# The first layer's row vectors, low halves, modulation sums and spatial gating in another order

## The chip, the core and the metric

The kernel runs on one core of one Trainium2 chip, as one program. The metric is device microseconds for one execution. Engines: PE is TensorE, DVE VectorE, ACT ScalarE, POOL GpSimd, SP SyncE, which issues nearly all DMAs. PSUM holds eight banks of 128 partitions by 512 floats.

## What is computed

The reference is a network of two blocks on 512 tokens of width 1024, with a context of 256 tokens. The first block has two layers. Only its first layer matters here ("ab" in the code), which runs on the tokens and, with the same weights, on the context:

```python
m = silu(c) @ w_mod + b_mod            # sh, sc, gt: 3 x 1024; once for c, once for c_ctx
h = x * (1 + sc) + sh                  # 512 tokens, and 256 of the context
z = h @ w_in                           # a, ga, u, v, gb: 5 x 512
ya = pool(a) * silu(ga)                # window sums over tokens, a 128x128 product per group, a scale
vn = per-head layer norm of v          # 4 heads of 128
yb = u * (w_s @ vn + b_s) * silu(gb)   # spatial gating, w_s 128x128 per head, in chunks of 128 tokens
x = layer_norm(ALPHA * x + gt * (concat(ya, yb) @ w_out))
```

The second layer ("cd": Fourier mixing and attention) takes its modulation `silu(c) @ w_mod` from the same c, with weights of its own. The second block is two rounds of a gated feed-forward, a mixing layer with three kinds of attention, and a second feed-forward.

## The kernel before, in words

**Layout and precision.** Activations lie with channels on partitions, `[128, 8, 512]`; the first layer's 768 tokens are 512 of x (tile `X`, high and low half) and 256 of the context (`C`). Every large product is three matmuls (`mm3`, L144): a number is split into a rounded high half and the rest, and high times high, high times low and low times high are added. A tile of weights, 128x1024 floats, is loaded by `wload` (L74) on SP into `ws` (two buffers), its high half is made by ScalarE (L92), and its low half by the engine `s.w_eng` (L93). `wnext` (L127) takes the next weight and loads up to four ahead; there are five buffers of high and low halves. In the first two layers `s.w_eng` is GpSimd, set at L517 and set back to VectorE at L1075.

**Jobs.** `wload` also works off a list `s.jobs`: for each weight loaded it adds `s.rate` (2.2) to a count and runs a job for each whole one (L94 to L97). In the first layer the jobs are the modulations that aren't needed at once: rows 16 to 23 of the first layer's (the gate gt) and all 24 of the second layer's. One job (`mod_dve`, L468) loads a 512 KB tile of weights into one of the spare buffers and has VectorE multiply it by a row of silu(c) laid out over all partitions and sum it up (L475), once for c and once for c_ctx, or once only.

**The order.** The source gives the dependences and a priority; the build works out from them one fixed order for each engine and for SP's queue. An instruction whose inputs are due early may so stand before ones that are written ahead of it, as far as its buffers allow. At run time no engine leaves its order.

**The first layer.** `ab` (L514) works in stages:

- Modulation and the projection of v, to about 64 us. For each of eight channel tiles k, `mods(k)` (L540) computes the rows k and 8+k of the modulation: on TensorE for the rows in `ON_PE` (eight small products and a bias, L548, L549), on VectorE with `mod_dve` for the others. `modx(k)` (L554) scales x. Then 18 matmuls with `ab_v` add tile k's share into six banks `pv`. The rows of silu(c) that `mod_dve` needs are loaded as `crow`, 2 x 512 KB, the same in each partition (L562 to L565).
- The norm of v (L598 to L610): six copies out of PSUM by ScalarE, 24 `bn_stats` and `bn_aggr`, one `rsqrt` of eight small steps (L194 to L202), and 24 instructions that subtract the mean and scale, all on VectorE.
- Spatial gating, g = 0 to 3 (L625 to L647). One projection (`proj`, L612) is 24 matmuls of 512 columns into one bank and 24 of 256 into a second one; the six `mm` banks hold three projections. The order is u of 0, gb of 0, u of 1, then for each g the product `pf` of vn and w_s into the two `t` banks (L637), the sum with b_s (L642), the product with u (L644), with silu of gb (L645), and the split into the halves of Y (L646).
- Pooling, g = 0 to 3 (L658 to L700): projections a and ga, window sums by repeated addition (L668), corrections at the edges, the difference with a (L681), its split, the product `pp` with pool_w (L689), taken one group later, the scale (L691) and a split.
- All remaining jobs, the biases of both modulations and the second layer's `gb` (L702 to L715).
- The output: eight tiles of 24 + 24 matmuls, added to x by VectorE (L508), with token sums on GpSimd (L512); the last three by segments, then the layer norm (L487), interleaved with these.

`mod_dve`'s buffers for jobs are parts of `xs` and `ctmp` that lie idle (L580 to L585, L652).

Of the kernel before, what the change touches and what calls it, by code (L numbers as in the profile page):

```python
# [9 lines left out]
F32 = mybir.dt.float32  # L10
# [3 lines left out]
ALU = mybir.AluOpType  # L14
# [7 lines left out]
ALPHA = 4.0 ** 0.25  # L22
ON_PE = (0, 8, 10, 13, 15)
HALF = (slice(0, 256), slice(256, 512))
# [7 lines left out]
class Net:  # L32
# [415 lines left out]
    def ab_weights(s):  # L448
        I = s.I
        for c in range(4):  # L450
            s.wpush(I["ab_v"][c], 1024)
        for i in (8, 12, 9, 13, 10, 14, 11, 15):
            s.wpush(I["ab_in"][i], 1024)
        s.wpush(I["pool_w"], 512)
        for i in (0, 4, 1, 5, 2, 6, 3, 7):
            s.wpush(I["ab_in"][i], 1024)
        for m in range(8):
            s.wpush(I["ab_out"][m], 1024)
# [55 lines left out]
    def ab(s):  # L514
        nc, tc, I = s.nc, s.tc, s.I
        s.psum(mm=range(6), t=(6, 7))
        s.w_eng = nc.gpsimd  # L517
        fbt = s.xp.tile([P, 4096], F32, tag="fb", name="fbt")
# [5 lines left out]
        C = [c_p.tile([P, 8, 256], F32R, tag="c" + t, name="c" + t) for t in "HL"]  # L524
        s.mods_start()
        b1 = c_p.tile([P, 16], F32, name="b1")
        nc.vector.tensor_copy(b1[:, 0:8], s.vec("ab_b", 0, 8))
        nc.vector.tensor_scalar(b1[:, 8:16], s.vec("ab_b", 8, 8), 1.0, None, op0=ALU.add)
        xs = s.xp.tile([P, 4096], F32, tag="x", name="xs")
        pv = [s.bank("pv") for _ in range(6)]  # L530

# [22 lines left out]
        def modx(k):  # L554
            st = xs[:, k % 5 * 768:k % 5 * 768 + 768]
            nc.sync.dma_start(st, I["x"][:, k])
            s.modulate(X, k, ALL, st[:, :T], s.ab_m[:, 8 + k, 0:1], s.ab_m[:, k, 0:1], st[:, :T])
            s.modulate(C, k, slice(0, 256), st[:, T:], s.ab_m[:, 8 + k, 1:2], s.ab_m[:, k, 1:2], st[:, T:])
# [3 lines left out]
        for v in range(2):  # L562
            row = fbt[:, v * 1024:(v + 1) * 1024]
            nc.sync.dma_start(row, I["crow"][:, v * 1024:(v + 1) * 1024])
            nc.scalar.activation(row, row, AF.Silu)  # L565
        modx(0)
        mods(1)
        for k in range(8):
            if k % 2 == 0:
                W = s.wnext(1)  # L570
            if k < 7:
                modx(k + 1)
            if k < 6:
                mods(k + 2)
            w = [x[:, k % 2 * T:(k % 2 + 1) * T] for x in W]
            for t in range(6):
                s.mm3(pv[t], tokx(k, t), w, k == 0, k == 7)
        mx.close()
        ctmp = c_p.tile([P, 2048], F32, tag="cx", name="ctmp")
        spare = []  # L580

        def buf():
            spare.append(spare.pop(0))
            return spare[-1]
        spare += [xs[:, 3072:], ctmp[:, :1024], ctmp[:, 1024:]]  # L585
        nc.sync.dma_start(s.ident, I["ident"])
        nc.sync.dma_start(fbt[:, 2048:2560], I["sgu_b"])
# [3 lines left out]
        with tc.tile_pool(name="y", bufs=1, reuse_waits="tile") as yp, tc.tile_pool(name="yt", bufs=1, reuse_waits="tile") as tp:  # L591
# [14 lines left out]
            rv = s.rsqrt(ve, 24, "sgu")  # L606
            for t in range(6):
                for h in range(4):
                    j = t * 4 + h
                    nc.vector.tensor_scalar(vn[:, t, h], vn[:, t, h], mv[:, j, 0:1], rv[:, j:j + 1], op0=ALU.subtract, op1=ALU.mult)  # L610

# [12 lines left out]

            u = proj()  # L625
            for g in range(4):
                gb = proj()
                if g < 3:
                    u2 = proj()
                if g == 0:  # L630
                    s.jobs = [(lambda i=i: s.mod_dve(s.ab_m, I["ab_mod"], i, 2, fbt, buf)) for i in range(16, 24)]
                    s.jobs += [(lambda i=i: s.mod_dve(s.cd_m, I["cd_mod"], i, 2 if i < 16 else 1, fbt, buf)) for i in range(24)]
                G = tp.tile([P, 768], F32, tag="G", name="G")
                t_ = tp.tile([P, 768], F32, tag="T", name="T")
                pf = s.bank("pf", "t"), s.bank("pf", "t")
                for c in range(6):
                    nc.tensor.matmul(pf[c // 4][:, c % 4 * P:(c % 4 + 1) * P], vn[:, c, g], fbt[:, 2560 + g * P:2560 + (g + 1) * P], start=True, stop=True)  # L637
                for i, sl in enumerate(PARTS):
                    n = sl.stop - sl.start
                    bs = fbt[:, 2048 + g * P:2048 + (g + 1) * P].unsqueeze(1).to_broadcast([P, n // P, P])  # L640
                    tt = t_[:, sl]
                    nc.vector.tensor_tensor(tt.rearrange("p (c i) -> p c i", i=P), pf[i][:, :n].rearrange("p (c i) -> p c i", i=P), bs, op=ALU.add)  # L642
                    nc.scalar.activation(G[:, sl], gb[i], AF.Silu)
                    nc.vector.tensor_tensor(tt, tt, u[i], op=ALU.mult)  # L644
                    nc.vector.tensor_tensor(tt, tt, G[:, sl], op=ALU.mult)  # L645
                    ysplit(4 + g, tt, sl)  # L646
                u = u2  # L647


            LP = 800  # L650
            A, S1, S2 = ctmp[:, 0:LP], ctmp[:, LP:2 * LP], fbt[:, 3072:3072 + LP]
            spare[:] = [xs[:, j * 1024:(j + 1) * 1024] for j in range(4)]  # L652
            nc.gpsimd.memset(ctmp, 0.0)
# [47 lines left out]

            while s.jobs:  # L702
                s.jobs.pop(0)()
            s.add_bias(s.ab_m, "ab_b", 16, 24)

            nc.vector.tensor_scalar(s.ab_m[:, 16:24], s.ab_m[:, 16:24], 1.0 / ALPHA, None, op0=ALU.mult)
            s.add_bias(s.cd_m, "cd_b", 0, 16)
            s.add_bias(s.cd_m, "cd_b", 16, 24, 1)
            nc.vector.tensor_scalar(s.cd_m[:, 8:16], s.cd_m[:, 8:16], 1.0, None, op0=ALU.add)

            s.gb = s.fc.tile([P, 2, 8, 2], F32, name="gb")
            for v in range(2):
                nc.vector.tensor_tensor(s.gb[:, 0, :, v], s.cd_m[:, 8:16, v], s.vec("ab_g", 0, 8), op=ALU.mult)
                nc.vector.tensor_tensor(s.gb[:, 1, :, v], s.cd_m[:, 8:16, v], s.vec("ab_lb", 0, 8), op=ALU.mult)
                nc.vector.tensor_tensor(s.gb[:, 1, :, v], s.gb[:, 1, :, v], s.cd_m[:, 0:8, v], op=ALU.add)  # L715
            ag = c_p.tile([P, 2, 8], F32, name="ag")
# [22 lines left out]
            for m in range(5):  # L739
                W = s.wnext()  # L740
                a, b = s.bank("pa"), s.bank("pb")[:, :256]
                omm(a, W, slice(0, T))
                omm(b, W, slice(T, 768))
                fin(m, 0, a[:, 0:256])
                fin(m, 1, a[:, 256:512])
                fin(m, 2, b)
            Ws = s.wlast(3)

# [751 lines left out]
def prep_first(inp, A, vec):  # L1500
    i = lambda n: inp[n][0]
    cc = np.stack([i("c"), inp["c_ctx"]])
    vec("c", np.ascontiguousarray(cc.reshape(2, 8, P).transpose(2, 1, 0)).reshape(P, 16))
    A["crow"] = np.ascontiguousarray(np.broadcast_to(cc.reshape(1, 2048), (P, 2048)))
    vec("ab_b", rows(i("ab_b_mod")))
# [130 lines left out]
```

## Time and profile before

| | us |
|---|---|
| median of 3 runs | 2746.2 |
| the runs | 2743.26, 2746.2, 2751.51 |
| the profiled execution's own time | 2743.77 |
| its span in the trace | 2741.7 |

In the profile TensorE is busy for 2632.7 us (96% of the span), VectorE for 1504.3, ScalarE for 1056.6, GpSimd for 323.0. A line of a timeline gives start, duration, engine, source line, operation, output<-inputs and, in brackets, how long the engine was idle before and what ended that. Matmul durations overlap: the pitch of two is shorter than one. DVE_READ_ACCUMULATOR rows belong to the sum before them. In the first 350 us the trace has 34 low halves on GpSimd and 78 sums on VectorE.

### The profile page before, as it was taken

How to read it: one execution, taken by the hardware profiler on the slowest of the kernel's cores; microseconds unless marked ns; L12 is line 12 of the kernel's file. 1: busy time of each engine (PE TensorE's matmuls, PEld its weight loads, DVE VectorE, ACT ScalarE, POOL GpSimd, SP SyncE). 2: the span in 40 equal slices, each digit the busy share in tenths (PEclk: the TensorE clock that was granted, in tenths of full speed). 3: DMA queues.
4: the chain of work that ended last, by engine and by line, in shares of the span. 5: the costliest groups of instructions: out<-in, count | busy, mean ns of one | idle time of the engine just before them, and what ended most of it. 6: DMA issues, size and time to landing. Idle time of an engine off the chain costs nothing. (4 is left out here: it accounts for less than half of the span.)

```text
span 2741.7 us, 36211 instructions
## 1 busy us (share of the span) xinstructions
PE 2632.7 (96%) x13676; PEld 2230.8 (81%) x13676; DVE 1504.3 (55%) x2886; ACT 1056.6 (39%) x1951; POOL 323.0 (12%) x300
## 2 busy tenths in 40 slices
PE   7898999998999999999999999999999998999998
PEld 6787987887888888878888888888888877988887
DVE  7895632888545345675853336633336666642434
ACT  4122533664444233454543224432223454432222
POOL 2323344003000011001200002000001001200000
PEclk9999999998999999999999999999999999999999
DMA  7353123004998247654693323963237655232221
GB/s 271 135 193 120 44 82 101 32 30 166 312 315 291 91 141 234 195 154 140 219 317 109 99 84 108 318 221 100 92 101 243 208 156 156 76 100 99 94 94 60
DMA packets 133966, 418.15 MB, mean 153 GB/s; under 512 B 17376, under 2 KB 20960, under 8 KB 133792
## 3 DMA queue, kind: packets, MB, share of 16 engines
q1 hardware_dynamic: 133792, 415.84, 45.7%
q8 instruction: 108, 1.77, 0.3%
q14 instruction: 66, 0.54, 0.1%
HBM read 314.32 MB, written 73.40 MB: 141 GB/s over the span
## 5 line engine op out<-in xcount | busy, mean ns | idle before, releaser
L92 ACT ACTIVATE wh<-ws 128x1024 fp32r<-128x1024 f32 (+2 forms) x335 | 345.3, 1033 | 865.4 <-PE pd L148 238.6
L93 DVE TENSOR_TENSOR wl<-ws,wh 128x1024 fp32r<-128x1024 f32 (+1 forms) x267 | 318.3, 1192 | 164.4 <-ACT wh L92 161.1
L147 PE MATMUL pg<-xH,wh 128*128 128x512 f32 x672 | 262.2, 390 | 0.0
L149 PE MATMUL pg<-xH,wl 128*128 128x512 f32 x672 | 261.7, 389 | 0.0
L148 PE MATMUL pg<-xL,wh 128*128 128x512 f32 x672 | 261.6, 389 | 0.0
L149 PE MATMUL pd<-hH,wl 128*128 128x512 f32 x632 | 249.6, 395 | 0.0
L147 PE MATMUL pd<-hH,wh 128*128 128x512 f32 x632 | 249.6, 395 | 0.0
L148 PE MATMUL pd<-hL,wh 128*128 128x512 f32 x632 | 249.6, 395 | 0.0
L148 PE MATMUL pu<-xL,wh 128*128 128x512 f32 x640 | 249.2, 389 | 0.0
L147 PE MATMUL pu<-xH,wh 128*128 128x512 f32 x640 | 249.1, 389 | 0.0
L149 PE MATMUL pu<-xH,wl 128*128 128x512 f32 x640 | 249.0, 389 | 0.0
L93 POOL TENSOR_TENSOR wl<-ws,wh 128x1024 fp32r<-128x1024 f32 (+1 forms) x68 | 171.5, 2529 | 326.1 <-ACT wh L92 317.0
L247 POOL TENSOR_TENSOR accf<-accf,sq 128x256 f32<-128x256 f32 x48 | 39.7, 847 | 1390.1 <-ACT sq L246 1390.1
L399 DVE TENSOR_TENSOR ht<-ht,pu 128x512 f32<-128x512 f32 x80 | 54.9, 686 | 182.5 <-PE pu L149 180.4
L149 PEld LDWEIGHTS pg<-xH,wl 128*128 128x128 f32 x672 | 126.1, 188 | 26.1
L148 PEld LDWEIGHTS pg<-xL,wh 128*128 128x128 f32 x672 | 126.2, 188 | 26.0
L147 PEld LDWEIGHTS pg<-xH,wh 128*128 128x128 f32 x672 | 126.2, 188 | 26.1
L148 PEld LDWEIGHTS pd<-hL,wh 128*128 128x128 f32 x632 | 118.6, 188 | 28.8
L149 PEld LDWEIGHTS pd<-hH,wl 128*128 128x128 f32 x632 | 118.6, 188 | 28.8
L147 PEld LDWEIGHTS pd<-hH,wh 128*128 128x128 f32 x632 | 118.6, 188 | 28.7
L147 PEld LDWEIGHTS pu<-xH,wh 128*128 128x128 f32 x640 | 120.1, 188 | 25.0
L148 PEld LDWEIGHTS pu<-xL,wh 128*128 128x128 f32 x640 | 120.1, 188 | 24.9
(622 smaller groups left out, 5982.6 us busy)
## 6 DMA issues: line engine op xcount, KB each, us to landing
ws<-ffn_gate SPq DMA_DIRECT2D x88, 512.0 KB, 3.5
ws<-ffn_up SPq DMA_DIRECT2D x88, 512.0 KB, 3.5
hl<-eh SPq DMA_DIRECT2D x64, 512.0 KB, 6.8
hl<-el SPq DMA_DIRECT2D x64, 512.0 KB, 6.8
ws<-ffn_down SPq DMA_DIRECT2D x64, 512.0 KB, 3.6
wh<-hl SPq DMA_DIRECT2D x58, 512.0 KB, 4.3
wl<-hl SPq DMA_DIRECT2D x58, 512.0 KB, 6.0
es<-wqk SPq DMA_DIRECT2D x32, 512.0 KB, 5.8
```

The source lines that it names most:

```text
L92: nc.scalar.activation(wh[:, :n], st[:, :n], AF.Copy)
L93: s.w_eng.tensor_tensor(wl[:, :n], st[:, :n], f(wh[:, :n]), op=ALU.subtract)
L147: mm(out, A[0], B[0], start=start, stop=False)
L148: mm(out, A[0], B[1], start=False, stop=False)
L149: mm(out, A[1], B[0], start=False, stop=stop)
L247: (eng or nc.gpsimd).tensor_tensor(acc[0], acc[0], sq, op=ALU.add)
L399: nc.vector.tensor_tensor(t, t, pu, op=ALU.mult)
```

## The change

It has six parts. `ON_PE` gets eight rows instead of five (rows 1, 9, 12 and 14 come in, 13 goes out). Low halves of the first two layers are made by VectorE. The rows of silu(c) are made on TensorE: sixteen products of a column of silu(c), taken as a weight matrix of equal columns, with the identity, copied out of four banks by ScalarE; the load of `crow` goes, the identity is loaded at the start. The scale of v by its norm goes head by head and is shared: odd token tiles on ScalarE, even ones on VectorE; the jobs' VectorE instructions are tied behind the last one on VectorE (`issue_after`), have three buffers of their own and a rate of 1.4. The spatial gating's product, sum and product with u of group g stand ahead of the projection gb of g, and the projections come as u0, u1, gb0, u2, gb1, u3, gb2, gb3. Up to 24 jobs and the second layer's `gb` may come behind the first five output tiles.

```diff
-ON_PE = (0, 8, 10, 13, 15)
+ON_PE = (0, 1, 8, 9, 10, 12, 14, 15)
@@ ab_weights
-        for i in (8, 12, 9, 13, 10, 14, 11, 15):
+        for i in (8, 9, 12, 10, 13, 11, 14, 15):
             s.wpush(I["ab_in"][i], 1024)
@@ ab
-        s.w_eng = nc.gpsimd
+        s.w_eng = nc.vector
...
         s.mods_start()
+        nc.sync.dma_start(s.ident, I["ident"])
...
-        pv = [s.bank("pv") for _ in range(6)]
...
         for v in range(2):
-            row = fbt[:, v * 1024:(v + 1) * 1024]
-            nc.sync.dma_start(row, I["crow"][:, v * 1024:(v + 1) * 1024])
-            nc.scalar.activation(row, row, AF.Silu)
+            for h in range(2):
+                pr = s.bank("pr")
+                for j in range(4):
+                    nc.tensor.matmul(pr[:, j * P:(j + 1) * P], s.sc[:, 4 * h + j, v:v + 1].to_broadcast([P, P]), s.ident, start=True, stop=True)
+                nc.scalar.activation(fbt[:, v * 1024 + h * T:v * 1024 + (h + 1) * T], pr, AF.Copy)
         modx(0)
+        s.wload(1)
         mods(1)
+        pv = [s.bank("pv") for _ in range(6)]
...
-        spare = []
-        def buf():
-            spare.append(spare.pop(0))
-            return spare[-1]
-        spare += [xs[:, 3072:], ctmp[:, :1024], ctmp[:, 1024:]]
-        nc.sync.dma_start(s.ident, I["ident"])
+        buf = lambda: c_p.tile([P, 1024], F32, tag="mj", name="mj", bufs=3)
...
             rv = s.rsqrt(ve, 24, "sgu")
-            for t in range(6):
-                for h in range(4):
+            nb = c_p.tile([P, 24], F32, name="nb")
+            nc.vector.scalar_tensor_tensor(nb, mv[:, :, 0], -1.0, rv, op0=ALU.mult, op1=ALU.mult)
+            for h in range(4):
+                for t in range(6):
                     j = t * 4 + h
-                    nc.vector.tensor_scalar(vn[:, t, h], vn[:, t, h], mv[:, j, 0:1], rv[:, j:j + 1], op0=ALU.subtract, op1=ALU.mult)
+                    if t % 2:
+                        nc.scalar.activation(vn[:, t, h], vn[:, t, h], AF.Identity, scale=rv[:, j:j + 1], bias=nb[:, j:j + 1])
+                    else:
+                        normed = nc.vector.tensor_scalar(vn[:, t, h], vn[:, t, h], mv[:, j, 0:1], rv[:, j:j + 1], op0=ALU.subtract, op1=ALU.mult)
...
-            u = proj()
+            def after_v(*a):
+                def run():
+                    with tc.issue_after(normed.ins):
+                        s.mod_dve(*a, fbt, buf)
+                return run
+            us = [proj(), proj()]
+            s.jobs = [after_v(s.ab_m, I["ab_mod"], i, 2) for i in range(16, 24)]
+            s.jobs += [after_v(s.cd_m, I["cd_mod"], i, 2 if i < 16 else 1) for i in range(24)]
+            s.rate = 1.4
             for g in range(4):
-                gb = proj()
-                if g < 3:
-                    u2 = proj()
-                if g == 0:
-                    s.jobs = [(lambda i=i: s.mod_dve(s.ab_m, I["ab_mod"], i, 2, fbt, buf)) for i in range(16, 24)]
-                    s.jobs += [(lambda i=i: s.mod_dve(s.cd_m, I["cd_mod"], i, 2 if i < 16 else 1, fbt, buf)) for i in range(24)]
-                G = tp.tile([P, 768], F32, tag="G", name="G")
-                t_ = tp.tile([P, 768], F32, tag="T", name="T")
                 pf = s.bank("pf", "t"), s.bank("pf", "t")
...
+                t_ = tp.tile([P, 768], F32, tag="T", name="T")
                 for i, sl in enumerate(PARTS):
...
                     nc.vector.tensor_tensor(tt.rearrange("p (c i) -> p c i", i=P), pf[i][:, :n].rearrange("p (c i) -> p c i", i=P), bs, op=ALU.add)
+                    nc.vector.tensor_tensor(tt, tt, us[g][i], op=ALU.mult)
+                gb = proj()
+                if g < 2:
+                    us.append(proj())
+                G = tp.tile([P, 768], F32, tag="G", name="G")
+                for i, sl in enumerate(PARTS):
                     nc.scalar.activation(G[:, sl], gb[i], AF.Silu)
-                    nc.vector.tensor_tensor(tt, tt, u[i], op=ALU.mult)
-                    nc.vector.tensor_tensor(tt, tt, G[:, sl], op=ALU.mult)
-                    ysplit(4 + g, tt, sl)
-                u = u2
+                    nc.vector.tensor_tensor(t_[:, sl], t_[:, sl], G[:, sl], op=ALU.mult)
+                    ysplit(4 + g, t_[:, sl], sl)
...
-            spare[:] = [xs[:, j * 1024:(j + 1) * 1024] for j in range(4)]
...
-            while s.jobs:
+            while len(s.jobs) > 24:
                 s.jobs.pop(0)()
             s.add_bias(s.ab_m, "ab_b", 16, 24)
...
                 fin(m, 2, b)
+            while s.jobs:
+                s.jobs.pop(0)()
```

Behind the last two lines stand, unchanged, the biases of the second layer's modulation and its `gb`, which stood behind the pooling before.

## Rows read from the trace of the kernel before

**Rows 1.** The page, its first line: the span and the number of instructions

```profile
span 2741.7 us, 36211 instructions
```

**Rows 2.** Busy time by stretch (us), instructions as (x), TensorE's granted clock, DMA share, GB/s

```profile
64.00:149.00 85.00, 77.51 (x422) 66.47 (x421) 66.83 (x148) 17.56 (x26) 31.90 (x12) 0.92 0.42 148
97.10:101.70 4.60, 4.58 (x12) 3.09 (x11) 4.50 (x8) 0.00 (x0) 0.00 (x0) 0.50 0.19 47
149.00:224.90 75.90, 72.78 (x417) 63.87 (x416) 73.07 (x117) 19.21 (x35) 19.94 (x7) 0.98 0.55 188
224.90:245.20 20.30, 10.16 (x46) 8.17 (x45) 16.32 (x20) 5.83 (x11) 7.86 (x3) 0.75 0.48 159
245.20:290.00 44.80, 44.80 (x283) 40.31 (x284) 9.62 (x22) 5.85 (x8) 19.41 (x17) 1.00 0.20 66
331.00:690.00 359.00, 341.34 (x1979) 293.41 (x1979) 221.07 (x481) 188.63 (x403) 92.94 (x63) 0.97 0.24 82
```

**Rows 3.** TensorE's timeline, 78 to 113 us: start, duration, line, tiles, [idle before <-releaser]

```profile
80.49 0.39 PE L147 MATMUL pa<-xH,wh 128*128 128x512 f32 x1
89.32 0.49 PE L637 MATMUL pf<-fbt,xs 128*128 128x128 f32 x2 [0.40 <-DVE xs L610]
92.52 0.80 PE L637 MATMUL pf<-fbt,xs 128*128 128x128 f32 x2 [2.72 <-DVE xs L610]
105.13 0.67 PE L147 MATMUL pa<-xH,wh 128*128 128x512 f32 x1 [3.45 <-DVE T L644]
```

**Rows 4.** VectorE's timeline, 60 to 130 us

```profile
66.88 1.68 DVE L603 BATCH_NORM_AGGREGATE mv<-bns 128x2 f32<-128x6 f32 x24
73.48 2.37 DVE L196 TENSOR_TENSOR tsgu<-ysgu 128x24 f32<-128x24 f32 x1
88.92 8.42 DVE L610 TENSOR_SCALAR xs<-xs,mv,ysgu 128x128 f32<-128x128 f32 x24
```

**Rows 5.** The sums' line L475 (min/median/max ns), and groups by line up to 350 us

```profile
L475 DVE CUSTOM_DVE_ANT_0 junk<-xs,fbt x42: 1212/1224/3455, 68.5 to 216.7; 128x1024 bf16<-128x1024 f32 x42
L475 DVE CUSTOM_DVE_ANT_0 junk<-xs,fbt 128x1024 bf16<-128x1024 f32 x42 | 65.0, 1549 | 1.6 <-DMA xs<-cd_mod 1.0
L475 DVE CUSTOM_DVE_ANT_0 junk<-wm,fbt 128x1024 bf16<-128x1024 f32 x22 | 33.0, 1501 | 0.2
```

**Rows 6.** TensorE's timeline, the end of the first and the start of the last pool product

```profile
184.22 0.28 PE L149 MATMUL pp<-yH,wl 128*128 128x256 f32 x1
...
238.10 0.80 PE L147 MATMUL pp<-yH,wh 128*128 128x512 f32 x1 [8.87 <-ACT yH L236]
```

**Rows 7.** VectorE's timeline, 184 to 240 us

```profile
197.56 1.14 DVE L691 SCALAR_TENSOR_TENSOR T<-pp,vecs,G 128x512 f32<-128x512 f32 x2
...
225.19 3.02 DVE L668 TENSOR_TENSOR ctmp<-ctmp 128x799 f32<-128x799 f32 x1 [0.98 <-ACT ctmp L663]
```

**Rows 8.** Timelines of VectorE and of TensorE in the first layer's layer norm

```profile
315.06 2.35 DVE L200 TENSOR_TENSOR tab<-yab 128x2 f32<-128x2 f32 x1
...
320.43 1.22 PE L217 MATMUL bcab<-ident,yab 128*128 128x128 f32 x4 [1.87 <-DVE yab L202]
```

**Rows 9.** The start: busy time in 5.5 to 12.5 us, and TensorE's timeline

```profile
5.50:12.50 7.00, 6.96 (x32) 6.87 (x32) 0.22 (x2) 2.11 (x2) 0.00 (x0) 1.00 1.01 392
...
19.21 0.80 PE L148 MATMUL pv<-wl,xH 128*128 128x512 f32 x1 [1.74 <-POOL wl L93]
...
37.52 0.50 PE L147 MATMUL pv<-wh,xH 128*128 128x512 f32 x1 [2.34 <-ACT xH L483]
```

**Rows 10.** The page, groups by line: the low halves that VectorE works out

```profile
L93 DVE TENSOR_TENSOR wl<-ws,wh 128x1024 fp32r<-128x1024 f32 (+1 forms) x267 | 318.3, 1192 | 164.4 <-ACT wh L92 161.1
```

**Rows 11.** Groups by line to 350 us; waits there (total us, times, longest)

```profile
L93 POOL TENSOR_TENSOR wl<-ws,wh 128x1024 fp32r<-128x1024 f32 (+1 forms) x34 | 91.7, 2706 | 175.8 <-ACT wh L92 169.9 <-PE pp L149 4.5 <-PE pb L148 1.3
...
ACT wh L92 <- PE pb L148: 44.7, 8, 7.4
```

**Rows 12.** ScalarE's timeline, 119 to 350 us

```profile
156.70 0.42 ACT L236 ACTIVATE yH<-T 128x256 fp32r<-128x256 f32 x1 [4.19 <-DVE T L645]
```

More of the change, by code (lines that the diff above doesn't have):

```diff
@@ L706, in ab @@
             nc.vector.tensor_scalar(s.ab_m[:, 16:24], s.ab_m[:, 16:24], 1.0 / ALPHA, None, op0=ALU.mult)
[L707 to L715, printed above, removed]
             ag = c_p.tile([P, 2, 8], F32, name="ag")
@@ L746, in ab @@
                 fin(m, 2, b)
+            while s.jobs:
+                s.jobs.pop(0)()
+            s.add_bias(s.cd_m, "cd_b", 0, 16)
+            s.add_bias(s.cd_m, "cd_b", 16, 24, 1)
+            nc.vector.tensor_scalar(s.cd_m[:, 8:16], s.cd_m[:, 8:16], 1.0, None, op0=ALU.add)
+            s.gb = s.fc.tile([P, 2, 8, 2], F32, name="gb")
+            for v in range(2):
+                nc.vector.tensor_tensor(s.gb[:, 0, :, v], s.cd_m[:, 8:16, v], s.vec("ab_g", 0, 8), op=ALU.mult)
+                nc.vector.tensor_tensor(s.gb[:, 1, :, v], s.cd_m[:, 8:16, v], s.vec("ab_lb", 0, 8), op=ALU.mult)
+                nc.vector.tensor_tensor(s.gb[:, 1, :, v], s.gb[:, 1, :, v], s.cd_m[:, 0:8, v], op=ALU.add)
             Ws = s.wlast(3)
@@ L1503, in prep_first @@
     vec("c", np.ascontiguousarray(cc.reshape(2, 8, P).transpose(2, 1, 0)).reshape(P, 16))
-    A["crow"] = np.ascontiguousarray(np.broadcast_to(cc.reshape(1, 2048), (P, 2048)))
     vec("ab_b", rows(i("ab_b_mod")))
```

## The prediction

> **What bounds the kernel now.** I read the page first: the span is 2741.7 us and the profiled execution took 2743.8 us [rows 1]; the sum below is made against the latter. The median of the three runs, 2746.2 us, stands 2.4 us above it, so the forecast for a median is set between the two. TensorE carries nearly the whole span, so a change in the first layer counts only as far as it takes TensorE's waits away, or adds to them. Hence the second view, busy time by stretch, over the first layer [rows 2].
>
> The reader should compare each stretch with its floor. One projection of 768 tokens is 48 matmuls and takes 8.3 us unhindered (80.49 to 88.92, where the wait before 89.32 begins, less the last one's overlap, [rows 3]). From 64 to 149 us stand eight projections and the gating's matmuls (48 instructions, 0.12 us each at full pace, 5.8 us): floor 72.2, span 85, so 12.8 lost. From 149 to 224.9 stand eight projections and three pool products of 1.05 us: floor 69.6, span 75.9, so 6.3 lost. From 224.9 to 245.2 TensorE ran 46 matmuls, some 0.18 us each: floor 8.3, so 12.0 lost. **Together 31 us**, 1.1% of the whole. From 245 to 290 nothing is lost, VectorE idling for 35 of 45 us; and in the attention layer (331 to 690) TensorE is 95% busy.
>
> Where the 31 us go is read from TensorE's timeline. (a) The gating's first product waits for the norm of v, then the fourth projection for the bank of the first (2.72 and 3.45 us), and after such gaps matmuls run with a granted clock of 0.50, the 1.2 GHz level [rows 2, 3]. (b) A pool product waits 8.87 us for its input [rows 6].
>
> Both come from VectorE's queue. It works in a fixed order: v's statistics end at 68.6, but the scale by the norm starts only at 88.9, because eight sums of later modulations (1.22 us and a 0.08 us read each) stand in that chain, and four tiny steps of it, like the one at 73.48, take 2.37 instead of 0.17 us [rows 4, 5]. Those four lie beside low halves running on GpSimd. The sums show the same: median 1.22, maximum 3.46 us [rows 5]. In the pool stage the lag can be seen whole: the first pool product ended at 184.5, its reader on VectorE started at 197.56, with VectorE busy all the while [rows 6, 7].
>
> **The change, part by part.**
>
> *Low halves on VectorE.* 34 low halves up to 350 us [rows 11], and those of the attention layer, leave GpSimd for VectorE, 1.19 us each [rows 10]: 40 us more up to 350. Back come the stretched instructions: 64 sums at means of 1.55 and 1.50 instead of 1.22 (20 us, [rows 5]), four norm steps (8.8), two pool additions (4), two steps of the layer norm (4.4, [rows 8]): 37 us. VectorE's load is about even, but the stalls sat in chains and the low halves do not: weights are taken four projections ahead, 33 us of cover. If that cover goes, rival 4 holds.
>
> *Sums behind the norm, spatial gating first (12.8 us).* Without the eight sums and stretches the norm chain is 9 small steps (1.8 us) and 24 scales, of which ScalarE takes 12: VectorE 12 x 0.35 = 4.2 us [rows 4], ScalarE 12 x at most 0.42, its 256-column row, [rows 12]. Even with two low halves between, the last scale ends 68.6 + 1.8 + 4.2 + 2.4 = 77. The product now stands after two projections: 63.9 + 16.6 = 80.5. So it waits for nothing, and the first bank is free during the third projection. New is that the fifth and seventh projections want a bank whose gating stands just ahead of them: product, add, multiply, 1.5 us each with 0 to 2 sums of 1.3 us between, unless TensorE has other matmuls queued there. I take 2.5 in all (0 to 8). Net gain 10 (bounds 5 and 12.8).
>
> *Jobs at 1.4 instead of 2.2 per weight, 24 of 32 allowed past the pools (18.3 us).* By the counting of the load loop 21 jobs (42 sums) are traced up to the last pool projection, seven more beside the first five output tiles, and four behind these: 14 sums, 18 us, against VectorE's 35 idle us there: no cost. In the pool stage that leaves VectorE 27 us of pool steps (ten additions of 0.95 us and 4.4 us of smaller steps for each of four groups), 10 low halves (12 us) and at most 26 sums (33 us): 72 of 70 us, against 89 in the trace [rows 2]. That is still full, so not all of the lag need go. But 13 us of lag become at most a few; a pool product stands 16.6 us after the step that its input hangs on, with some 7 us of chain in it. At the hand-over, the four additions shrink from 8 to 4 us [rows 7], and TensorE has the first output tiles to fill with. I take a gain of 13 (bounds 2 and 18).
>
> *Rows of c on TensorE.* Removed are two loads of 512 KB from a queue running at 392 GB/s [rows 9], 2.6 us for whatever follows. Added: 16 products of a broadcast column with the identity, 32 instructions: 3.8 us at full pace (0.12), 9.8 at the slow one (1.22 us for 4, [rows 8]), of which some 2 us lie ahead of the first weight's arrival at 5.5. Three more modulations on TensorE cost some 1.8 us each (32 instructions for two took 6.96 us at the slow pace, [rows 9]); those of step 1 fit between 12.5 and 19.2, where it stood nearly empty. The first low half takes 1.19 instead of some 3 us, and it held the real start until 19.21 [rows 9]. VectorE loses six sums and the stretches; TensorE's wait of 2.34 us [rows 9] for a modulation shrinks. Sum -2.6 + 3 - 1.9 + 4 - 2 = 0.5; I take 0 (bounds -6 and +5).
>
> *Layer norm and the attention layer.* TensorE waited 1.87 us at 320.4 behind two stretched steps [rows 8]; three low halves (3.6 us) come into VectorE's queue instead. I take -1.5 (-4.4 to +2). From 331 to 690 VectorE is 62% busy [rows 2] and TensorE is fed: 0 (-3 to +3). The 24 scales' split, the later addition of biases and the freed buffers hang beside work already counted: 0, the cover being the idle VectorE from 245 to 290.
>
> **Sum:** 0 - 10 - 13 - 1.5 + 0 = -24.5, so 2719.3 us for this execution; I give **2719 us**. All good bounds: -44, 2700. All bad ones: +3, 2747.
>
> What a page says against this: the Trainium skill, "TensorE: Matmul & The Clock Gate", section on the second failure mode, tells of a kernel whose short waits between groups of matmuls, cycling through PSUM banks, let the clock fall and rise again and again. The trace shows both: after the wait of 2.34 us the next matmul took 0.50 us [rows 9], after one of 2.72 us a pair took 0.80 instead of 0.49 [rows 3]. By the first row the new bank waits cost their own length, as the sum has it; by the page they would cost a slow stretch each as well (rival 2).
>
> **Rivals.** (1) *VectorE stays full.* The sums are ready whenever their buffer is, and the order may put them ahead of pool steps as before; 72 us of work for 70 says so. Then the pool stage's 18.3 us stay but for the 4 of the additions: -10 - 4 - 1.5 = 2728. Against it: 17 us less work in that stage.
>
> (2) *The new waits bring the clock down.* Three places (fifth and seventh projection, first pool projection), each 2 us of wait and 1.7 to 2.1 us at half pace as around 97 to 109 us, instead of 2.5 in all: 9.5 us less gain, 2729. Against it: the 2.34 us without a fall.
>
> (3) *The change does not do what it says.* The tie holds back the sums only; the order of everything else is the build's, and in the trace instructions stand far from their place in the source. If the gating's product stays behind the third projection, or the scales on ScalarE stand behind a conversion that waits for TensorE (ScalarE spent 44.7 us in eight such waits, [rows 11]), the gating gives 1 and the pools 4: 2739.
>
> (4) *Slower: VectorE inherits GpSimd's wait.* GpSimd waited 169.9 us for high halves, which wait for TensorE to let a weight go [rows 11]. A low half on VectorE waits in order: whatever stands behind it, the gating's add that frees a bank among them, waits for a projection to end, while TensorE waits for the bank. It decides if a low half stands directly ahead of a bank's reader and its high half comes later than TensorE's need. Price: per projection an add, a multiply and a sum (0.69 + 0.69 + 1.26 = 2.6 us) over 16 projections, 42 us, against the 31 gone: +11, 2755. Against it: the order is built so that a low half's source is due by then, and VectorE already carries 267 low halves of the later layers [rows 10].
>
> **How the numbers follow.** Forecast 0.55, rival 1 0.18, rival 2 0.08, rival 3 0.12, rival 4 0.07. The range 2705 to 2737 takes in the forecast with most of its bounds and rivals 1 and 2, and leaves out rival 4, most of rival 3 and the outer ends, 0.2. A measurement tells apart 0.3%, 8.2 us: faster means below 2738. Faster 0.55 + 0.18 + 0.08 + 0.02 = 0.83; same 0.10; slower 0.07.
>
> **What would show it.** Right: no sum between the statistics and the last scale on VectorE; gating products without a wait before 85 us; sums at 1.22 us throughout; the pool products' waits under 1 us; the first output tile begun some 22 us earlier against the end of v's projection. Wrong: a granted clock of 0.5 in the gating; waits of pool products on VectorE as before; v's projection ending after 68 us; VectorE waiting for high halves with a bank's reader behind.

## The result, and the profile after

The changed kernel takes 2712.5 us (median of 4 runs, 2709.8 to 2715.9) beside 2746.7 for the kernel before on the same chip: ratio 0.9875 [0.9855, 0.9895], 34.2 us or 1.25% faster. The profiled execution took 2710.3 us against 2743.8, its span 2708.5 against 2741.7 [rows 1]. The first line of the page after, and busy time by stretch: from the end of v's projection 85 us as in [rows 2], then up to the first output tile, the whole pool stage (which overlaps the two before it in the list), the next 20.3 and 44.8 us as in [rows 2], and from there to the products of the second layer's Fourier branch (`pf`). The columns are TensorE, its weight loads, VectorE, ScalarE, GpSimd, granted clock, DMA share, GB/s.

```profile
span 2708.5 us, 36337 instructions
```

```profile
66.60:151.60 85.00, 83.54 (x495) 73.75 (x494) 82.71 (x183) 26.48 (x45) 0.00 (x0) 1.00 0.65 207
151.60:209.40 57.80, 57.80 (x341) 51.36 (x340) 50.02 (x98) 16.64 (x29) 0.00 (x0) 1.00 0.51 166
140.30:209.40 69.10, 69.10 (x403) 61.22 (x402) 61.18 (x117) 20.32 (x35) 0.00 (x0) 1.00 0.58 187
209.40:229.70 20.30, 20.30 (x114) 17.36 (x113) 13.22 (x22) 7.94 (x15) 2.17 (x3) 1.00 0.43 137
229.70:274.50 44.80, 44.58 (x312) 41.65 (x311) 19.10 (x47) 6.64 (x13) 8.53 (x11) 1.00 0.13 43
274.50:318.40 43.90, 42.75 (x349) 41.21 (x348) 31.87 (x94) 32.98 (x68) 16.49 (x20) 1.00 0.13 43
```

TensorE lost 31 us between 64 and 245 before [rows 2]. Now it idles for 1.5 in the first stretch and not at all from there to 229.7, with the clock granted in full. VectorE is fuller than it was in the first stretch (82.7 of 85 us; 66.8 before) and less full in the second (50.0 of 57.8; 73.1 of 75.9 before), and TensorE waits for it once, for 1.5 us. All of TensorE's larger waits up to 345 us (total, times, longest):

```profile
PE pr L566 <- DMA ident<-ident: 3.3, 1, 3.3
PE pm L548 <- DMA wm<-ab_mod: 1.8, 1, 1.8
PE pa L147 <- DVE T L649: 1.5, 1, 1.5
PE pv L147 <- ACT xH L483: 1.2, 2, 0.7
```

By the timelines the 33.2 us of the span came as follows. v's projection ends at 66.8 instead of 64.1: +2.7. The first output tile begins at 209.6 instead of 224.9, so gating and pools give 18.0. The first column sum of the layer norm stands at 275.2 instead of 302.9: 12.3 more, the hand-over. From there to the first product `pf` of the second layer it takes 43.28 instead of 47.13 us: 3.9. The remaining 1.7 come later.

VectorE's norm chain after, and its sums (count: min/median/max ns):

```profile
70.96 1.19 DVE L93 TENSOR_TENSOR wl<-ws,wh 128x1024 fp32r<-128x1024 f32 x1
73.48 0.18 DVE L196 TENSOR_TENSOR tsgu<-ysgu 128x24 f32<-128x24 f32 x1
75.11 3.17 DVE L613 TENSOR_SCALAR xs<-xs,mv,ysgu 128x128 f32<-128x128 f32 x12
78.19 1.21 DVE L475 CUSTOM_DVE_ANT_0 junk<-mj,fbt 128x1024 bf16<-128x1024 f32 x1
```

```profile
L475 DVE CUSTOM_DVE_ANT_0 junk<-mj,fbt x56: 1210/1218/1228, 78.2 to 188.8; 128x1024 bf16<-128x1024 f32 x56
```

The step that took 2.37 us [rows 4] takes 0.18, the scales start at 75.1 instead of 88.9, the first sum follows the last scale, and no sum exceeds 1.23 us where the longest was 3.46 [rows 5]. All 56 sums of the jobs are done by 190.0 us, 19.5 before the first output tile: 31 stand in the gating stage and 25 in the pool stage, where it was 24 and 32 before. So no job came late, although the change allows 24 to. TensorE's gating: the first product without a wait, and the one wait for a bank.

```profile
83.14 1.50 PE L642 MATMUL pf<-fbt,xs 128*128 128x128 f32 x12
...
106.05 0.50 PE L147 MATMUL pa<-xH,wh 128*128 128x512 f32 x1 [1.46 <-DVE T L649]
```

### The profile page after: what moved, and what is told of

Read it like the earlier page. It is cut to its first block, busy times and chain, and to the rows that moved or that the text cites. A ratio compares the mean times of both kernels' runs of the same rounds, so it can differ in the third digit from the quotient of the medians.

```text
span 2708.5 us, 36337 instructions
## 1 busy us (share of the span) xinstructions
PE 2627.8 (97%) x13756; PEld 2231.8 (82%) x13756; DVE 1507.5 (56%) x2923; ACT 1062.9 (39%) x1965; POOL 172.3 (6%) x240
## 4 chain that ended last, share of the span: by engine, by line
PE 82%; DVE 10%; ACT 4%; DMA 2%; issue 2%; SPq 0%; POOL 0%; DVEq 0%; ACTq 0%; POOLq 0%
PE pd L148 6%; PE pd L149 6%; PE pd L147 6%; PE pg L147 5%; PE pg L149 5%; PE pg L148 5%; PE pu L149 5%; PE pu L148 5%; PE pu L147 5%; PE pa L147 1%; PE pa L149 1%; PE pa L148 1%; DVE x L313 1%; PE pq L147 1%; PE pq L148 1%
## 5 line engine op out<-in xcount | busy, mean ns | idle before, releaser
L93 DVE TENSOR_TENSOR wl<-ws,wh 128x1024 fp32r<-128x1024 f32 (+2 forms) x327 | 390.0, 1194 | 219.4 <-ACT wh L92 213.5
L149 PEld LDWEIGHTS pu<-xH,wl 128*128 128x128 f32 x640 | 120.1, 188 | 25.1
L237 DVE TENSOR_TENSOR el<-es,eh 128x1024 fp32r<-128x1024 f32 x64 | 78.2, 1223 | 103.6 <-DMA hl<-el 69.3
```

What stands on the lines that cost most here:

```text
L93: s.w_eng.tensor_tensor(wl[:, :n], st[:, :n], f(wh[:, :n]), op=ALU.subtract)
L149: mm(out, A[1], B[0], start=False, stop=stop)
L237: s.nc.vector.tensor_tensor(L, src, f(H), op=ALU.subtract)
```

## The experiments

The change has several parts, and the traces alone cannot say which of them paid. Theory A: low halves on GpSimd lengthen VectorE's instructions beside them, and that is the loss. Theory B: the order of sums and gating is. Each ratio below is to the kernel before on the same chip in the same session (medians 2743.5 to 2744.4). The last column is read from one profiled execution of each run, and the granted clock moves it: e5 has the instructions of the changed kernel in the same order up to there, and v's projection ends at 69.0 in one and 66.8 in the other, with a granted clock of 0.93 and 0.97 over that stretch.

| run | median us | ratio [95%] | v's projection ends |
|---|---|---|---|
| e1: the change, low halves on GpSimd | 2745.2 | 1.0007 [0.9997, 1.0016] | 75.0 |
| e2: before, low halves on VectorE | 2706.0 | 0.9865 [0.9850, 0.9879] | 63.9 |
| e3: the change, its start undone | 2709.6 | 0.9875 [0.9860, 0.9890] | 64.2 |
| e5: the change, gating in the old order | 2711.8 | 0.9884 [0.9869, 0.9898] | 69.0 |
| e13: e3, low halves on GpSimd | 2738.5 | 0.9983 [0.9970, 0.9995] | 69.2 |
| e8: e2 with spare subtractions on GpSimd | 2751.8 | 1.0034 [1.0021, 1.0047] | 71.4 |
| e9: e2 with spare copies on GpSimd | 2728.8 | 0.9948 [0.9933, 0.9964] | 67.1 |
| e10: e2, first weight earlier | 2708.9 | 0.9880 [0.9863, 0.9896] | 64.0 |
| e14: e2, two more rows on TensorE | 2706.9 | 0.9870 [0.9852, 0.9888] | 65.8 |
| e3b: the change, five rows on TensorE | 2714.2 | 0.9891 [0.9873, 0.9908] | 71.0 |
| e12: e2, GpSimd's adds on VectorE too | 2694.0 | 0.9819 [0.9803, 0.9835] | 63.4 |
| e16: e12, rows of c first, on TensorE | 2691.6 | 0.9804 [0.9791, 0.9818] | 61.8 |

### One line undone, one line done (e1, e2)

```diff
 # e1, in the changed kernel; e2 is the reverse in the kernel before
-        s.w_eng = nc.vector
+        s.w_eng = nc.gpsimd
```

> The changed kernel with one part undone: the first two layers' low halves back on GpSimd. Theory A (the low halves beside VectorE's work are the main cause: they stretch its sums and short steps, and VectorE's queue lags): sums at a mean of 1.5 instead of 1.22 us, steps of 2.4 us in the norm chain, waits of pool products on VectorE again, 12 to 20 us slower than the changed kernel: 2725 to 2733. Rival B (the order of the sums and of the gating did it; VectorE's load is the same either way): within 4 us of the changed kernel, 2709 to 2717, with stretched sums that nobody waits for.

> The kernel before with one part done alone: the first two layers' low halves on VectorE. Theory A: pool stage and hand-over lose less, the gating's wait for the norm stays (eight sums still stand in that chain, now unstretched): 10 to 18 us faster than before, 2729 to 2737. Rival B: 40 us more work for VectorE where it was full, paid back by 37 us of stretches: within 4 us of the kernel before, 2743 to 2751.

**e1** gives the whole gain back, more than theory A expected (2725 to 2733); part of that lies in the start, where v's projection ends at 75.0 instead of 66.8. Its sums by line, two low halves on GpSimd with a step of the norm that has one tensor as input and ends with the second (82.03 and 82.00), and TensorE's waits from 64 to 345 us:

```profile
L475 DVE CUSTOM_DVE_ANT_0 junk<-mj,fbt 128x1024 bf16<-128x1024 f32 x56 | 83.0, 1482 | 3.0 <-DMA mj<-cd_mod 2.1
```

```profile
77.25 4.75 POOL L93 TENSOR_TENSOR wl<-ws,wh 128x1024 fp32r<-128x1024 f32 x2 [9.71 <-ACT wh L92]
80.18 1.85 DVE L603 TENSOR_SCALAR ve<-mv 128x24 f32<-128x24 f32 x1
```

```profile
PE pa L147 <- DVE T L649: 11.1, 3, 6.0
PE pf L642 <- DVE T L648: 4.2, 1, 4.2
```

The new bank waits that the prediction had feared as rival 2 are here, up to 6.0 us long, and so is the slow clock: behind one of 4.55 us the granted clock is 0.50 from 105 to 110 us. **e2**, that single line in the kernel before, takes 37.7 us off, also more than expected, and lies level with the whole change: the two intervals overlap. Its stretches from v's end on, and the norm's end in the timelines of VectorE and TensorE:

```profile
63.90:149.00 85.10, 85.10 (x502) 75.07 (x502) 78.47 (x184) 21.08 (x32) 1.81 (x1) 1.00 0.50 170
149.00:205.10 56.10, 56.10 (x333) 49.94 (x332) 55.19 (x109) 16.72 (x29) 0.00 (x0) 1.00 0.63 207
205.10:225.40 20.30, 20.30 (x113) 17.18 (x112) 13.15 (x22) 7.78 (x15) 2.17 (x3) 1.00 0.54 179
```

```profile
81.38 6.25 DVE L610 TENSOR_SCALAR xs<-xs,mv,ysgu 128x128 f32<-128x128 f32 x24
```

```profile
88.53 1.50 PE L637 MATMUL pf<-fbt,xs 128*128 128x128 f32 x12
```

TensorE is busy without a gap, though VectorE is 98% busy in the pool stage (55.2 of 56.1 us), and though six sums and four low halves still stand between the statistics and the scales. With every instruction at its own length the norm is done at 87.6 instead of 97.3, a microsecond before the product in its old place wants it. So neither the tie nor the new place of the gating was needed.

### The other parts (e3, e5, e13)

e3 loads the rows of c again and returns to five rows on TensorE; e5 returns to u, gb, u of the next group, then the product; e13 is e3 with `s.w_eng = nc.gpsimd`.

```diff
 # e3
-ON_PE = (0, 1, 8, 9, 10, 12, 14, 15)
+ON_PE = (0, 8, 10, 13, 15)
...
+            nc.sync.dma_start(row, I["crow"][:, v * 1024:(v + 1) * 1024])
+            nc.scalar.activation(row, row, AF.Silu)
```

> The changed kernel with the start undone: the rows of silu(c) loaded as before and five rows of the modulation on TensorE. If rows of c on TensorE cost what the two traces show (v's projection ended 2.7 us later), 2 to 4 us faster than the changed kernel, 2708.5 to 2710.5, with v's projection ending near 64. Rival: the six sums that come back delay VectorE ahead of the norm, and it is as fast or up to 5 us slower, 2712 to 2718.

> The changed kernel with the spatial gating in its old order (u, gb, u of the next group, then the product with the norm), its tie, low halves and all else kept. Theory A: the norm is done near 80 us, before the product's old place at 89, so nothing waits for it in either order: within 3 us of the changed kernel, 2709.5 to 2715.5. Rival C (the order itself frees the banks): TensorE waits 2 to 4 us for banks behind the first products, as before, with a stretch at a granted clock of 0.50: 8 to 11 us slower, 2720 to 2723.

> The changed kernel with low halves back on GpSimd and the rows of c loaded as before: what is left are the tie, the gating's new order, the split of the scales, the job rate and the late jobs. With low halves on VectorE these parts gave nothing (2709.6 against 2706.0). Theory A: on GpSimd they shorten the norm's chain and give a few us of the gating's 12.8 back, the pool stage stays as before: 2735 to 2742. Rival B (they carry the gain when the start does not spoil it): 2715 to 2725.

e3 ends v's projection at 64.2, as expected, and its 2.9 us less than the changed kernel lie within the two intervals. The gating's order is worth nothing measurable: e5 lies on the changed kernel. With low halves on GpSimd the other parts give 5.2 us (e13), as expected in size but not in place: the gating was to gain and the pools to stay as before (and v's projection ends 5 us later than before). Its stretches from v's end on show the pool stage free already, while the gating loses 15 us:

```profile
69.00:154.00 85.00, 69.56 (x382) 60.61 (x381) 78.62 (x156) 19.28 (x33) 22.98 (x10) 0.90 0.51 171
154.00:232.00 78.00, 77.60 (x454) 68.68 (x453) 67.99 (x106) 22.79 (x40) 24.51 (x9) 1.00 0.50 169
```

With these parts the pool stage holds 17 of the 56 sums, where it held 32 before, and the last one ends at 201.2, 31 us before the first output tile: no job came late here either. So the pools could be had in two ways; the gating only by taking the low halves off GpSimd. Tie and rate were not tried apart.

### Is it GpSimd's mere presence? (e8, e9)

e2 may win because VectorE's instructions are no longer lengthened, or because low halves come earlier or in a better order (rival D). e8 leaves e2's instructions and their order on VectorE and TensorE untouched and adds, beside each low half of the first two layers (60 in all), a GpSimd subtraction whose result nobody reads; e9 a copy. In the traces all three runs have the same instructions of TensorE, VectorE and ScalarE in the same order.

```diff
 # e8; e9 has nc.gpsimd.tensor_copy(s.jp[:, :n], f(wh[:, :n]))
             s.w_eng.tensor_tensor(wl[:, :n], st[:, :n], f(wh[:, :n]), op=ALU.subtract)
+            if s.spare_op:
+                nc.gpsimd.tensor_tensor(s.jp[:, :n], f(wh[:, :n]), f(wh[:, :n]), op=ALU.subtract)
```

> The kernel before with low halves on VectorE, and beside each low half of the first two layers a spare subtraction of the same size on GpSimd, from the high half into a tile that nobody reads. VectorE's and TensorE's instructions and their order are exactly those of the run without the spare ones (2706.0). Theory A (GpSimd's work lying beside VectorE's stretches VectorE's instructions, whoever needs it): sums at means above 1.4 us and short steps of over 2 us return, the last scale by v's norm ends behind 93 us, and it is 20 us or more slower than without: 2726 to 2755. Rival D (the loss came from GpSimd's low halves being late for TensorE, or from the order that the build made with them): nothing waits for the spare work, within 4 us of 2706.

> As the run with spare subtractions, with a spare copy of the high half in their place: one input instead of two. If any GpSimd work beside VectorE stretches it by the time that GpSimd takes, the loss is that of the subtraction scaled by the duration of one: more than 10 us slower than 2706. If it takes two tensors read at once, within 4 us of 2706, with sums at 1.22 us.

The useless subtractions cost 45.8 us against e2 and make it slower than the kernel before: it has VectorE's low halves and the lengthening too. Rival D falls. The spare work reads the weight's high half, and so could hold its buffer; but TensorE's waits for high halves up to 560 us are 3.8 and 0.9 us in e8 as in e2. The mechanism can be read to the hundredth in e8's timelines of GpSimd (jp) and VectorE:

```profile
83.03 1.90 POOL L96 TENSOR_TENSOR jp<-wh 128x1024 f32<-128x1024 f32 x1 [5.91 <-ACT wh L93]
83.10 1.87 DVE L201 SCALAR_TENSOR_TENSOR tsgu<-tsgu 128x24 f32<-128x24 f32 x1
84.89 1.21 DVE L94 TENSOR_TENSOR wl<-ws,wh 128x1024 fp32r<-128x1024 f32 x1
85.13 2.73 POOL L96 TENSOR_TENSOR jp<-wh 128x1024 f32<-128x1024 f32 x1 [0.20 <-ACT wh L93]
86.03 1.87 DVE L202 SCALAR_TENSOR_TENSOR ysgu<-tsgu,ysgu 128x24 f32<-128x24 f32 x1
```

A step of 24 columns, 0.18 us alone, starts just behind GpSimd's subtraction and ends with it (84.97 and 84.93). The next subtraction starts while VectorE's low half runs, ends 0.83 us late, and the following step ends with it again (87.90 and 87.86). In these rows the engines take turns by whole instructions: the price is not set by the VectorE instruction's size but by what is left of GpSimd's. A longer one pays the same: a low half that starts just behind a subtraction takes 2.91 us instead of 1.21. e8's sums by line, and its low halves by line and as min/median/max ns:

```profile
L478 DVE CUSTOM_DVE_ANT_0 junk<-xs,fbt 128x1024 bf16<-128x1024 f32 x42 | 56.0, 1332 | 0.3
L94 DVE TENSOR_TENSOR wl<-ws,wh 128x1024 fp32r<-128x1024 f32 x32 | 50.7, 1583 | 3.6 <-ACT wh L93 3.6
L94 DVE TENSOR_TENSOR wl<-ws,wh x34: 691/1218/2911, 19.3 to 341.9; 128x1024 fp32r<-128x1024 f32 x32, 128x512 fp32r<-128x512 f32 x2
```

The sums were expected above 1.4 us and stay below; here it is the low halves (1.24 in e2) that meet the spare work, which is released by the same high half. A copy on GpSimd takes 1.04 us where nothing holds it, and lengthens a step to 1.02 (e9, GpSimd and VectorE):

```profile
77.68 1.07 POOL L96 COPY jp<-wh 128x1024 f32<-128x1024 f32 x1 [6.35 <-ACT wh L93]
77.77 1.01 DVE L201 SCALAR_TENSOR_TENSOR tsgu<-tsgu 128x24 f32<-128x24 f32 x1
```

Half the duration, half the loss: 22.8 us for e9 against 45.8. It does not take two inputs on GpSimd's side. The Trainium skill, "SBUF — State Buffer", section "Who interferes with whom", states that VectorE with two inputs in SBUF contends with a GpSimd instruction that reads SBUF, and that the second to issue blocks for the whole of the first. The rows above agree, in both directions.

Not every VectorE instruction is held. The statistics of v, with one tensor as input, take as long in e8 beside GpSimd's subtractions (first two rows; a third subtraction starts at 73.26) as in e2 with GpSimd idle (last row):

```profile
68.46 2.87 POOL L96 TENSOR_TENSOR jp<-wh 128x1024 f32<-128x1024 f32 x1 [13.64 <-ACT wh L93]
69.77 4.74 DVE L606 BATCH_NORM_STATS2 bns<-xs 128x6 f32<-128x128 f32 x24 [0.19 <-ACT xs L604]
62.28 4.73 DVE L601 BATCH_NORM_STATS2 bns<-xs 128x6 f32<-128x128 f32 x24
```

### The start (e10, e14, e3b)

```diff
 # e10, in e2
         modx(0)
+        s.wload(1)
 # e14, in e2
-ON_PE = (0, 8, 10, 13, 15)
+ON_PE = (0, 4, 8, 10, 12, 13, 15)
 # e3b, in the changed kernel
-ON_PE = (0, 1, 8, 9, 10, 12, 14, 15)
+ON_PE = (0, 8, 10, 13, 15)
```

> The kernel before with low halves on VectorE (2706.0) and the first weight's load put ahead of the second modulation. There TensorE waited 3.8 us for the first high half, which stood behind the first scale of x on ScalarE, and 1.7 us for the low half. If that was what held the start: v's projection ends 2 to 4 us earlier than 63.5, 2702 to 2704. If the modulations' loads hold it: no change, 2704 to 2708.

> The kernel before with low halves on VectorE (2706.0) and rows 4 and 12 of the modulation on TensorE too, seven in all. There VectorE was busy for 42 of the 48 us from 16 to 64, TensorE for 43.6. If VectorE holds the start: four sums (5 us) go, v's projection ends 2 to 3 us earlier than 63.5, 2702 to 2704. If TensorE does: two times 8 small products of 0.12 to 0.22 us come in, 2 to 3 us later, 2708 to 2710.

> The changed kernel (2712.5, v's projection ends at 66.6) with its rows of c made on TensorE, but the old five rows of the modulation there. With both undone it took 2709.6 and v's projection ended at 63.8. If the three more rows of the modulation are what costs (three times some 1.8 us on TensorE): back to 64 and 2709 to 2710. If the rows of c themselves do (32 instructions that stand ahead of the first modulation): stays at 66 to 67 and 2711 to 2714.

e10 moved nothing: ScalarE still made the first high half behind the scales of x, and TensorE's wait of 3.8 us stayed. e14 put v's end 1.9 us later, no more than e5 and the changed kernel differ, at no measurable cost in the whole: more rows on TensorE show no gain in a start in which VectorE is no longer lengthened. e3b answers against the guess that the three added rows cost the 2.7 us: without them v's projection ends at 71.0, later than either expectation, so they were a repair, and the rows of c are the cost. With five rows it lies in VectorE's sums, which begin late; the first one in e3b and in the changed kernel:

```profile
18.74 1.22 DVE L475 CUSTOM_DVE_ANT_0 junk<-wm,fbt 128x1024 bf16<-128x1024 f32 x1
```

```profile
25.48 1.22 DVE L475 CUSTOM_DVE_ANT_0 junk<-wm,fbt 128x1024 bf16<-128x1024 f32 x1
```

In e2 it starts at 12.5. The products that make the rows stand behind and between the first modulations on TensorE (in the changed kernel 24 of the 32 instructions from 13.92 us on), so in e3b the sums begin 6.2 us late, and v's projection ends 7.1 us later than in e2. The 25.5 of the changed kernel does not compare as it stands: the rows 1 and 9, with which VectorE begins in e2, are on TensorE there. It is bound otherwise, as the stretch up to v's end and TensorE's instructions for the modulations and for the rows of c show:

```profile
0.00:66.80 66.80, 60.58 (x305) 53.78 (x306) 38.10 (x97) 31.40 (x48) 2.71 (x6) 0.97 0.71 263
L548 PE MATMUL pm<-sc,wm 128*128 128x2 f32 x128 | 18.7, 277 | 1.8 <-DMA wm<-ab_mod 1.8
L566 PE MATMUL pr<-ident,sc 128*128 128x128 f32 x32 | 7.9, 434 | 3.3 <-DMA ident<-ident 3.3
```

VectorE is busy for 38.1 of 66.8 us, TensorE for 60.6, and from 5.8 us on it idles for only 1.2. There its own work sets the end.

### Beyond both kernels (e12, e16)

e12 carries the finding on: it is e2 with the other two-tensor work of GpSimd on VectorE too, mainly sums of squares in the tails of later layers. e16 is e12 with the rows of c on TensorE, ahead of the first modulation.

```diff
 # e12
-            (eng or nc.gpsimd).tensor_tensor(acc[0], acc[0], sq, op=ALU.add)
+            (eng or nc.vector).tensor_tensor(acc[0], acc[0], sq, op=ALU.add)
...
-            (nc.gpsimd if m < 5 else nc.vector).tensor_tensor(acc, acc, vm, op=ALU.add)
+            nc.vector.tensor_tensor(acc, acc, vm, op=ALU.add)
...
 # and in mix()
-        s.w_eng = nc.gpsimd
+        s.w_eng = nc.vector
```

> The kernel before with low halves on VectorE (2706.0), and all other two-tensor work of GpSimd moved to VectorE as well: the sums of squares (132 adds of 0.83 us in the later layers, six in the first layer's norm), the token sums (20), and the eight low halves of the mixing layers. Theory A carried on: in the tails TensorE waits on VectorE's short steps (3.4 us for a rsqrt of the feed-forward, 3.6 and 2.7 for two others, some 25 us in all), and these steps are stretched by the adds; 5 to 15 us faster, 2691 to 2701. Rival E: VectorE is then the one chain in the tails (an add of some 0.4 us per square in its queue), and what is no longer stretched is spent on them: within 4 us of 2706, or slower.

> The run with no adds on GpSimd (2694.0; rows of c loaded, v's projection ends at 63.4), with the rows of silu(c) made on TensorE ahead of the first modulation, five rows of the modulation on TensorE as before. In the changed kernel these products stood behind and between the first modulations, and VectorE's first sum started at 25.5 us (18.7 with five rows) instead of 12.5. If the late sums are what the rows of c cost: first sum at or before 12.5, v's projection ends at 62 to 64, 2691 to 2695. If the products on TensorE themselves cost it: v's projection ends at 66 or later, 2696 to 2701.

e12 gains another 12.0 us, and its interval lies below e2's. A step of the feed-forward's rsqrt over the whole run, in e2 and in e12 (busy us, mean ns):

```profile
L199 DVE SCALAR_TENSOR_TENSOR yffn_post<-tffn_post,yffn_post 128x2 f32<-128x2 f32 x8 | 2.9, 364 | 0.1
```

```profile
L199 DVE SCALAR_TENSOR_TENSOR yffn_post<-tffn_post,yffn_post 128x2 f32<-128x2 f32 x8 | 1.3, 157 | 0.1
```

GpSimd took 0.83 us for an add that VectorE does in 0.42. So e12 does two things at once, the adds are shorter and nothing is lengthened by them; how the 12.0 us divide is not shown. In e16 the first sum starts at 9.2 and v's projection ends at 61.8, 1.6 us before e12's, so the rows of c on TensorE cost nothing once they stand first; that they pay is not shown, since the whole (2.4 us less) is within the two intervals. At 2691.6 us e16 is 2.0% below the kernel before, and its interval lies below that of the change.

```profile
3.23 5.38 PE L563 MATMUL pr<-ident,sc 128*128 128x128 f32 x32 [3.23 <-DMA ident<-ident]
```

```profile
9.18 1.22 DVE L475 CUSTOM_DVE_ANT_0 junk<-wm,fbt 128x1024 bf16<-128x1024 f32 x1 [5.28 <-DMA wm<-ab_mod]
```

## Why the prediction was right, and where not

The forecast was 2719 us, 24.5 less than the profiled execution of before; that fell by 33.5. The place of the loss was right: the 31 us of [rows 2], lost behind VectorE's queue. Term by term:

- **Spatial gating:** gain 10 predicted; 11.3 came (12.8 lost before, 1.5 after). Its signs were met: no sum between the statistics and the last scale, the first product unhindered at 83.1 (80.5 predicted; v's end stood 2.7 later). The first output tile, put some 22 us earlier against v's end, came 18.0 earlier. The bank waits were put at 2.5 us; one of 1.5 came.
- **Pools and hand-over:** 13 predicted, bounds 2 and 18; nothing is lost there any more, so all 18.3 came, just past the better bound. VectorE's work in the pool stage was counted well, 72 us against some 69 in the trace; but the instructions overlap at their ends, and it is busy for 61.2 of 69.1 us. The step that failed is the value taken for the lag: "that is still full, so not all of the lag need go". No product waited, and in e2, where VectorE is busy for 55.2 of 56.1 us, none did either. A queue whose instructions keep their length can be full without being late: the busy share did not measure the lag. The 14 sums that were to come beside the output tiles came in the gating stage, and cost nothing there.
- **Layer norm and the rest:** -1.5 predicted; 3.9 up to `pf` and 1.7 later came, inside the bounds. TensorE's wait of 1.87 us and the slow stretch behind it [rows 8] went with the stretched steps.
- **Start:** 0 predicted; +2.7 came, inside the bounds. The sum has 3 us for the rows of c and 4 for the three more modulations; TensorE spent 7.9 and 6.2 on them (18.7 for eight rows, 12.5 for five before). All its work up to v's end rose by 11.1 us, and its idle time there fell from 14.7 to 6.2. The working also calls the stretch of 6.96 us one at the slow pace, but its row gives a granted clock of 1.00 [rows 9]; what doubles the time of an instruction there is not shown. That the sums wait for the rows of c was not in the sum at all; it costs where five rows stay on TensorE (e3b).

The larger error is in the attribution, and the total hid it: that the sum came within 9 us of the gain is partly luck. The working took the load of the low halves' move as even (40 us of work for 37 us of stretches) and credited the gains to the tie, the order and the job rate. The runs show the reverse: the move alone gives 37.7 us, everything else without it nothing (e1) or 5.2 (e13). The text had the reason in one clause, "the stalls sat in chains and the low halves do not", but gave it no term of its own.

Rival 1 (VectorE stays full) fell: 61.2 of 69.1 us in the pool stage, and nothing lost there. Rival 2 (new waits bring the clock down) fell: one wait of 1.46 us, granted clock 1.00 throughout that stretch; what the Trainium skill, "TensorE: Matmul & The Clock Gate", section on the second failure mode, tells of did not occur here. With the low halves on GpSimd it would have come: e1 has the waits and the clock of 0.50. Rival 3 (the order is not as the source says) fell by the timeline, with the first sum right behind the last scale. Rival 4 (VectorE inherits GpSimd's wait) fell too: no bank or product waited longer than 1.5 us.

## What to carry to other kernels

When tiny VectorE instructions take microseconds, look at what GpSimd runs at that moment before reordering anything: an engine that "helps" with off-path work can lengthen the instructions that are on the path, as it did here, one whole instruction at a time. Equal sums of work are no argument for a neutral move; ask which of the two sits in chains. And price a step that makes an operand by its first reader as well as by its own engine, and ask which of the two engines has time to spare.

## What the runs showed of the hardware

GpSimd's fp32 subtractions and copies and VectorE's instructions with two tensors (sums, low halves, short steps) held each other up for whole instructions, in either direction: work that nobody reads cost 45.8 us, 1.7% of the whole. The statistics of v were not held (4.74 us in e8, 4.73 in e2). A VectorE step with a single tensor as input (`ve`, 24 columns) was held, though, 1.85 us in e1; the Trainium skill, "SBUF — State Buffer", section "Who interferes with whom", states that `tensor_scalar` can contend in its two-port modes. The row agrees that it was held; the mode it ran in is not shown. GpSimd was no cheap helper either: a subtraction of 128x1024 takes it 1.90 us where it isn't held (e8), VectorE 1.21.
